# One half of the first layer's modulation: from VectorE dot products to TensorE matmuls

## The chip, the cores and the metric

The kernel runs on one core of one Trainium2 chip (trn2). Times are device microseconds of one execution of the program. The kernel before was timed in three runs: 722.38 us median, 721.82 to 723.79. One further execution was recorded by the hardware profiler. Engines: TensorE (PE, its weight loads PEld), VectorE (DVE), ScalarE (ACT), GpSimd (POOL), and SyncE (SP), whose queue issues nearly all loads here.

## What is computed

Two layers over 256 tokens of width 1024, in fp32: a first layer with a recurrent mixer (hgrn2 and a short convolution), a second with sparse attention, each followed by a gated feed-forward network with a convolution. Every norm is modulated by a vector that comes from a condition `c`:

```python
c_act = jax.nn.silu(c)
for l in range(DEPTH):
    mod = c_act @ mod_w[l] + mod_b[l]
    sh1, sc1, g1, sh2, sc2, g2 = jnp.split(mod[:, None, :], 6, axis=-1)
    hm = rmsnorm(x, norm_mix_g[l]) * (1.0 + sc1) + sh1
...
    x = x + g1 * y
    hf = rmsnorm(x, norm_ffn_g[l]) * (1.0 + sc2) + sh2
    x = x + g2 * conv_ffn(hf, ffn_w_up[l], ffn_conv_w[l], ffn_w_down[l])
return rmsnorm(x, final_norm_g)
```

`mod_w` is 1024 x 6144 for each layer. What the change touches is `sc2` of the first layer: 1024 of these columns.

## The kernel before, in words

Activations are kept transposed: `xT` holds the 1024 features as 8 chunks of 128 partitions by 256 tokens. Every large product is done in three passes of matmuls (`Group.chunk`, L418 to L427, all recorded at L402): each operand is split into a high half (`fp32r`) and a low half, and high x high, low x high and high x low are added. A `Group` makes 256 output features in one PSUM tile `pg`; four chunks of 128 input features are 24 matmuls.

**Weights.** `Stream` reads all weights in the order of use. A dry run of the program writes down the order in which it asks for loads (`load`, L125), and the real run issues them in that order on SP's queue (`_dma`, L117 to L123) as soon as one of 6 buffers of 1 MB is free. Weights (`raw_w`) and modulation matrices (`raw_m`) share these buffers. A weight tile is split in pieces of four chunks: the high half on ScalarE (`whi`, L152), the low half on VectorE (`wlo`, L161), up to three pieces ahead of the matmuls, with four buffers for each half. A buffer is given back after its last low half (`lows`), after the second dot on it, or after the step of matmuls on it (`done`).

**Modulation.** A half is 1024 of the 6144 columns (two quarters of 512). There are two ways to make one:

- `mod_half` (L264 to L300) on TensorE, eight entries: four steps, each with a load of its own of 256 rows of two quarters and four matmuls of 128 x 32 by 512 columns into four column strips of one PSUM tile (`pm`, L283); a copy to SBUF on ScalarE (`mrow`, L289); an empty entry; four transposes (L294); two additions on VectorE (L298, L299).
- `mod_dots` (L302 to L315) on VectorE, eight entries: each one dot product of 128 output columns over all 1024 rows (L311, `raw_m` times `cb`, the condition on every partition). Two share a load.

**Order.** All engines run their instructions in the order of the program text (`manual_schedule`). What is not on the main line is put between: `defer` (L350) hands functions to later slots, and `side` is a list of background entries. `slot(n)` (L357) runs what is due, adds n to a credit of at most 2 and takes entries from `side` while the credit is 1 or more. A slot stands after a piece's splits and before its matmuls. `flush()` runs all that is left.

**The stretch in question**, 108 to 180 us, is the end of the first mixer. `chained` (L799) runs eight groups of the input projection with the recurrence between them. Then four output groups are computed over chunks 4 to 7 (L849 to L856): before each, `o_out(i)` (L782) transposes one head of `on` into the one PSUM tile of tag `a` (`pt`, L785), and after it `finish` forms `og` on VectorE (L789), its high half `ohi` on ScalarE (L790) and its low half `olo` (L791). As `pt` has one buffer, the next transpose waits for `og`. Then the same four groups run over chunks 0 to 3 (L858 to L866), with residuals into `xT` (L542), squares (L479, L481 `sqa`, L489 `sql`) and, in `out_tail` (L544), 24 recorded matmuls of one column each that sum the squares over partitions (L469, `pn`). `fill()` places the first entries of a half of the second layer (`mod_half(1, 0, 1)`) in the gaps: one step before the row sums, one after them, one after the spread of the result (`pb`, L502). Then the feed-forward network starts with the first matmuls on the normed input `hhi` (L513, L514).

Of the kernel before, what the change touches and what calls it, by code (L numbers as in the profile page):

```python
# [195 lines left out]
def model(ctx, tc, xt, pack, wts, rel_bias, k_f, k_mask, k_hot, out, plan, got):  # L196
# [67 lines left out]
    def mod_half(l, qa, qb, tag="m"):  # L264

        def cols(t):
            a = t[:, 4 * qa:4 * qa + 4]
            return bass.AP(tensor=a.tensor, offset=a.offset, ap=[list(a.ap[0]), [4 * (qb - qa), 2], [1, 4]])
        dst, bias = cols(modc[l]), cols(modb[l])
        s_ = {}  # L270

        def load(j):
            s_["i"] = st.load("m", 2048, "mod", l, 2 * j, 2, (512 * qa, 512 * qb), 512)
            return st.raw(s_["i"]).rearrange("p (k n) -> p k n", k=2)

        def pe_step(j):
            raw = load(j)
            if j == 0:
                s_["p"] = ps.tile([P, 512], "pm", tag)
            for e in range(2):  # L280
                for q in range(2):
                    o = 64 * e + 32 * q
                    pe.matmul(s_["p"][o:o + 32, :], cst[:, 2 * j + e, :], raw[:, e, q * 512:(q + 1) * 512],  # L283
                              start=(j == 0), stop=(j == 3), skip_group_check=True, tile_position=(0, o))
            st.done(s_["i"])

        def rows():
            s_["w"] = tmp.tile([P, 512], F32, name="mrow", bufs=1)
            act.activation(s_["w"], s_["p"], AF.Copy)  # L289

        def turn():
            s_["t"] = ps.tile([P, 4, P], "pm2", "m")
            for i in range(4):
                pe.transpose(s_["t"][:, i, :], s_["w"][:, i * P:(i + 1) * P], ident)  # L294

        def add():
            pv = s_["t"].rearrange("p j (e q r) -> p e q j r", q=2, r=32)
            dve.tensor_tensor(dst, pv[:, 0, :, :, 0], bias, op=OP.add)  # L298
            dve.tensor_tensor(dst, pv[:, 1, :, :, 0], dst, op=OP.add)  # L299
        return [lambda j=j: pe_step(j) for j in range(4)] + [rows, nop, turn, add]  # L300

    def mod_dots(l, q):  # L302

        s_ = {}

        def dot(j, e):
            if e == 0:
                s_["i"] = st.load("m", 2048, "dots", l, 512 * q + 256 * j)
            raw = st.raw(s_["i"])[:, e * D:(e + 1) * D]
            n = 4 * q + 2 * j + e  # L310
            dve.tensor_tensor_reduce(raw, raw, cb, scale=1.0, scalar=modb[l][:, n:n + 1], op0=OP.mult, op1=OP.add,  # L311
                                     accum_out=modc[l][:, n:n + 1])
            if e == 1:
                st.done(s_["i"])
        return [lambda j=j, e=e: dot(j, e) for j in range(4) for e in range(2)]  # L315
# [32 lines left out]
    due, side, credit = [], [], [0.0]  # L348
# [444 lines left out]

    chain = [diagonal] + [lambda h=h: level(h) for h in (1, 2, 4, 8, 16, 32, 64)] + [cross, o_products]
    after = [None]
    side.extend(mod_half(0, 4, 5) + mod_dots(0, 6) + mod_dots(0, 8))
    side[:0] = [nop] * 3

    def chained(G):  # L799
# [597 lines left out]
def trace(nc, consts, plan):  # L1397

    args = []
    for name, shape in list(_SHAPES.items()) + [(k, a.shape) for k, a in consts.items()]:  # L1400
        dt = mybir.dt.from_np(consts[name].dtype) if name in consts else F32
        args.append(nc.dram_tensor(f"in_{name}_dram", shape, dt, kind="ExternalInput").ap())
    out = nc.dram_tensor("out_0_dram", (1, S, D), F32, kind="ExternalOutput").ap()
    got = []
    try:
        with tile.TileContext(nc) as tc:
            model(tc, *args, out, plan, got)
    except Traced:
        pass
    return got[0].loads, got[0].subs  # L1410
# [13 lines left out]
```

## Time and profile before

| | us |
|---|---|
| median of three runs (lowest to highest) | 722.38 (721.82 to 723.79) |
| the profiled execution: its own time | 722.53 |
| span in the profile, first to last instruction | 720.8 |
| TensorE busy | 689.8 (96%) |
| VectorE busy | 517.0 (72%) |
| ScalarE busy | 372.9 (52%) |
| mean granted TensorE clock | 0.975 |

A profile is one execution. Busy shares are averages over stages with different limits, so the table of stretches is read before the shares. Matmuls are pipelined: a row's mean duration is longer than the step from one to the next, and the time of a run of them is read from the chain of waits or from the first and the last start. A granted clock of 1.0 is TensorE's level of 2.4 GHz, 0.5 its level of 1.2 GHz. An fp32 matmul of the modulation stands as two records, so a step of four is x8.

### The profile page before, as it was taken

The page shows a single profiled execution, that of the slowest core. Times are in us where ns is not written, and L with a number is a line of the kernel's source. Part 1 is how long each engine was busy: PE and PEld are TensorE (multiplying, and loading weights), DVE is VectorE, ACT ScalarE, POOL GpSimd, SP SyncE. Part 2 cuts the span into 40 slices and gives each one's busy share as a digit, 9 for nine tenths or more (in the row PEclk, how much of TensorE's full clock was granted, in tenths as well). Part 3 has the DMA queues.
Part 4 walks back from the last instruction along what each step waited for, and adds up shares of the span by engine and source line. Part 5 has one row for each costly group of instructions (what it writes and reads, how often), then busy time and mean ns, then how long its engine had stood idle before and what let it go on. Part 6 is the DMA issues. An engine that isn't in the chain of part 4 may idle for free.

```text
span 720.8 us, 14050 instructions
## 1 busy us (share of the span) xinstructions
PE 689.8 (96%) x5730; PEld 651.6 (90%) x5730; DVE 517.0 (72%) x954; ACT 372.9 (52%) x641; POOL 48.2 (7%) x80
## 2 busy tenths in 40 slices
PE   7999999696999999999999999999899999999996
PEld 4889899694999999999989799888799999999996
DVE  3658767866689989985558768788698977665452
ACT  5546245424555555534346668783564555453442
POOL 0000000000000000000010015665000000000000
PEclk9999999896999999999999999999899999999998
DMA  9996835976767878786558592516455865544201
GB/s 326 403 411 241 298 128 171 353 277 235 247 219 270 295 266 321 282 329 205 195 218 318 199 340 75 205 48 234 175 213 211 330 246 185 185 181 162 103 1 60
DMA packets 27793, 165.10 MB, mean 229 GB/s; under 512 B 3258, under 2 KB 3770, under 8 KB 10320
## 3 DMA queue, kind: packets, MB, share of 16 engines
q1 hardware_dynamic: 26352, 159.94, 60.4%
q0 software_dynamic: 944, 3.60, 1.5%
q8 instruction: 45, 0.74, 0.4%
q10 hardware_dynamic: 432, 0.66, 0.3%
q14 instruction: 20, 0.16, 0.1%
HBM read 163.10 MB, written 1.08 MB: 228 GB/s over the span
## 4 chain that ended last, share of the span: by engine, by line
PE 84%; DVE 7%; ACT 5%; DMA 2%; issue 1%; SPq 0%; POOL 0%; ACTq 0%; DVEq 0%
PE pg L402 71%; DVE wlo L161 2%; PE pl L715 2%; ACT whi L152 2%; DVE raw_m L311 2%; PE pm L283 2%; PE pn L469 1%; PE po L1051 1%; PE p L1021 1%; PE pc L1159 1%; PE pm L327 1%; DMA xT<-in_xt_dram 1%; PE sc L973 1%; DMA raw_w<-in_wts_dram 1%; ACT E L1005 1%
## 5 line engine op out<-in xcount | busy, mean ns | idle before, releaser
L161 DVE TENSOR_TENSOR wlo<-raw_w,whi 128x1024 fp32r<-128x1024 f32 (+1 forms) x194 | 227.0, 1176 | 118.5 <-ACT whi L152 117.4
L402 PE MATMUL pg<-hhi,whi 128*128 128x256 f32 x1096 | 296.1, 285 | 1.5 <-ACT hhi L514 1.3
L402 PE MATMUL pg<-hlo,whi 128*128 128x256 f32 x1096 | 291.2, 280 | 0.0
L402 PE MATMUL pg<-hhi,wlo 128*128 128x256 f32 x1096 | 287.9, 279 | 0.0
L152 ACT ACTIVATE whi<-raw_w 128x1024 fp32r<-128x1024 f32 (+1 forms) x194 | 195.4, 1016 | 147.6 <-PE pg L402 123.7
L402 PEld LDWEIGHTS pg<-hhi,whi 128*128 128x128 f32 x1096 | 199.9, 189 | 13.2 <-issue 6.7
L402 PEld LDWEIGHTS pg<-hlo,whi 128*128 128x128 f32 x1096 | 200.4, 189 | 0.0
L402 PEld LDWEIGHTS pg<-hhi,wlo 128*128 128x128 f32 x1096 | 197.6, 188 | 0.0
L402 PE MATMUL pg<-Ah,whi 128*128 128x256 f32 x352 | 99.7, 283 | 0.0
L402 PE MATMUL pg<-Ah,wlo 128*128 128x256 f32 x352 | 99.6, 283 | 0.0
L402 PE MATMUL pg<-Al,whi 128*128 128x256 f32 x352 | 98.7, 280 | 0.0
L311 DVE CUSTOM_DVE_ANT_0 raw_m<-raw_m,cb,pk 128x1024 f32<-128x1024 f32 x56 | 70.9, 1276 | 0.0
L402 PEld LDWEIGHTS pg<-Al,whi 128*128 128x128 f32 x352 | 67.0, 190 | 0.0
L402 PEld LDWEIGHTS pg<-Ah,whi 128*128 128x128 f32 x352 | 66.1, 188 | 0.0
L402 PEld LDWEIGHTS pg<-Ah,wlo 128*128 128x128 f32 x352 | 65.8, 187 | 0.0
L1012 POOL TENSOR_SCALAR E<-E,rr,gr 128x128 f32<-128x128 f32 (+1 forms) x64 | 41.3, 656 | 30.7 <-DVE rr L1010 22.0
L887 DVE SCALAR_TENSOR_TENSOR tt<-pg,pk,tt 128x255 f32<-128x255 f32 (+1 forms) x88 | 36.2, 473 | 2.9 <-ACT tt L883 2.9
L897 ACT ACTIVATE Ah<-tt 128x512 fp32r<-128x512 f32 x22 | 13.9, 633 | 46.2 <-DVE tt L896 46.2
L514 ACT ACTIVATE hhi<-xn,modc 128x256 fp32r<-128x256 f32 x31 | 15.1, 505 | 26.0 <-DVE xn L513 26.0
L1005 ACT ACTIVATE E<-E,mx 128x128 f32<-128x128 f32 (+1 forms) x64 | 28.2, 446 | 0.0
L889 ACT ACTIVATE tt<-tt 128x512 f32<-128x512 f32 x22 | 13.9, 633 | 15.0 <-DVE tt L887 14.6
L1086 POOL MEMSET bls<- 128x128 f32 x1 | 0.2, 204 | 310.8 <-PE pg L402 310.8
(231 smaller groups left out, 795.0 us busy)
## 6 DMA issues: line engine op xcount, KB each, us to landing
raw_w<-in_wts_dram SPq DMA_DIRECT2D x84, 1024.0 KB, 4.9
raw_m<-in_wts_dram SPq DMA_DIRECT2D x52, 1024.0 KB, 6.1
raw_e<-in_wts_dram SPq DMA_DIRECT2D x24, 256.0 KB, 9.0
raw_w<-in_wts_dram SPq DMA_DIRECT2D x8, 768.0 KB, 5.2
FDM<-ub POOLq DMA_DIRECT2D x4, 800.0 KB, 7.3
raw_w<-in_wts_dram SPq DMA_DIRECT2D x5, 512.0 KB, 5.6
xT<-in_xt_dram SPq DMA_DIRECT2D x3, 256.0 KB, 6.5
out_dram<-yo ACTq DMA_DIRECT2D x2, 256.0 KB, 2.9
```

Of the source, the lines that this page charges most:

```text
L152: self.nc.scalar.activation(hi, raw, AF.Copy)
L161: self.nc.vector.tensor_tensor(lo, raw, hi, op=OP.subtract)
L283: pe.matmul(s_["p"][o:o + 32, :], cst[:, 2 * j + e, :], raw[:, e, q * 512:(q + 1) * 512], start=(j == 0), stop=(j == 3), skip_group_check= ...
L311: dve.tensor_tensor_reduce(raw, raw, cb, scale=1.0, scalar=modb[l][:, n:n + 1], op0=OP.mult, op1=OP.add, accum_out=modc[l][:, n:n + 1])
L402: pe.matmul(o, a, b, start=self.first[i], stop=False, skip_group_check=True)
L514: act.activation(hi[:, k, :], xs[k], AF.Identity, bias=B[:, k:k + 1])
L715: pe.matmul(pp[:, hd, :], lhs[:, hd, ls * P:(ls + 1) * P], rhs[:, hd, rs * P:(rs + 1) * P], start=True, stop=True)
L887: dve.scalar_tensor_tensor(tt[:, m, d:], acc[:, m, :S - d], w_fc[l][:, c:c + 1], tt[:, m, d:], op0=OP.mult, op1=OP.add)
L889: defer(taps, lambda: act.activation(tt, tt, AF.Silu))
L897: act.activation(Ah[:, sl, :], tt, AF.Copy)
L1005: act.activation(o, o, AF.Exp, bias=E["mx"][:, t, br:br + 1], scale=-1.0, accum_out=E["den"][:, t, br:br + 1])
L1012: pool.tensor_scalar(o, o, rr[:, t, br:br + 1], gr4[:, t, 1 + br, n:n + 1], op0=OP.mult, op1=OP.mult)
```

## The change

The second half of modulation made in this stretch, quarters 8 and 9 of the first layer (columns 32 to 39 of `modc0`, `sc2`), goes from `mod_dots` to `mod_half`:

```diff
@@ -793,7 +793,7 @@
 
     chain = [diagonal] + [lambda h=h: level(h) for h in (1, 2, 4, 8, 16, 32, 64)] + [cross, o_products]
     after = [None]
-    side.extend(mod_half(0, 4, 5) + mod_dots(0, 6) + mod_dots(0, 8))
+    side.extend(mod_half(0, 4, 5) + mod_dots(0, 6) + mod_half(0, 8, 9))
     side[:0] = [nop] * 3
 
     def chained(G):
```

Both fill eight entries of `side` (one of the new eight is empty), at the same slots. Three places show what moves.

VectorE, over the output groups (`wlo` is the low half of a weight piece, `og` the head that the transposes wait for); minus is before, plus the change:

```order
 L161 TENSOR_TENSOR wlo<-raw_w,whi 128x1024
-L311 ISA raw_m,modc_81<-raw_m,cb,pk 128x1024
-L311 ISA modc_81 128x1
 L789 SCALAR_TENSOR_TENSOR og<-pt,pk,sg 128x256
 L791 TENSOR_TENSOR olo<-og,ohi 128x256
```

A dot stood between the low half and `og` of each of the four heads; it is gone four times, and four more dots are gone between there and `sqa` (two ahead of the first residual, one behind each of the first two residuals).

TensorE, at the same place, ahead of each head's transpose:

```order
 L402 MATMUL pg<-hhi,whi 128x256
 L402 MATMUL pg<-hlo,whi 128x256
 L402 MATMUL pg<-hhi,wlo 128x256
+L283 MATMUL pm<-raw_m,cst 32x512 x4
 L785 MATMUL pt<-kf,on 128x128 x2
 L402 MATMUL pg<-ohi,whi 128x256
```

A step of four matmuls now stands ahead of each of the four transposes; the four transposes of `mrow` (L294) stand behind the first group of the second round, its two additions on VectorE behind the first residual.

SP's queue of loads, before (`raw_w_1379` and `raw_w_1448` hold the weights of the four output groups for chunks 4 to 7, `raw_w_1514` and `raw_w_1585` those for chunks 0 to 3, 1738 and 1742 the first of the feed-forward network):

```order
L121 DMA raw_m_1387<-in_wts_dram 128x2048
L121 DMA raw_w_1448<-in_wts_dram 128x2048
L121 DMA raw_m_1453<-in_wts_dram 128x2048
L121 DMA raw_w_1514<-in_wts_dram 128x2048
L121 DMA raw_m_1518<-in_wts_dram 128x2048
L121 DMA raw_m_1550<-in_wts_dram 128x2048
L121 DMA raw_w_1585<-in_wts_dram 128x2048
L121 DMA raw_m_1625<-in_wts_dram 128x2048
L121 DMA raw_m_1662<-in_wts_dram 128x2048
L121 DMA raw_m_1701<-in_wts_dram 128x2048
L121 DMA raw_w_1738<-in_wts_dram 128x2048
L121 DMA raw_w_1742<-in_wts_dram 128x2048
```

The same places of the queue with the change (`raw_w_1453`, 1550, 1585, 1677 and 1718 are now the five weight loads):

```order
L121 DMA raw_m_1387<-in_wts_dram 128x2048
L121 DMA raw_m_1448<-in_wts_dram 128x2048
L121 DMA raw_w_1453<-in_wts_dram 128x2048
L121 DMA raw_m_1514<-in_wts_dram 128x2048
L121 DMA raw_m_1518<-in_wts_dram 128x2048
L121 DMA raw_w_1550<-in_wts_dram 128x2048
L121 DMA raw_w_1585<-in_wts_dram 128x2048
L121 DMA raw_m_1593<-in_wts_dram 128x2048
L121 DMA raw_m_1634<-in_wts_dram 128x2048
L121 DMA raw_m_1671<-in_wts_dram 128x2048
L121 DMA raw_w_1677<-in_wts_dram 128x2048
L121 DMA raw_w_1718<-in_wts_dram 128x2048
```

The number and the size of the loads are the same. The weights of the third and fourth output group are one place later, those of the second round's first two groups two places later, and all four loads of the half come before them.

## Rows read from the trace of the kernel before

**Rows 1.** The page's part 1: engine, busy us (share of span), instructions.

```profile
PE 689.8 (96%) x5730; PEld 651.6 (90%) x5730; DVE 517.0 (72%) x954; ACT 372.9 (52%) x641; POOL 48.2 (7%) x80
```

**Rows 2.** Busy time by stretch; the columns are named in its first line.

```profile
core 0: us, PE busy (x) PEld busy (x) DVE busy (x) ACT busy (x) POOL busy (x), PEclk, DMA share, GB/s
112.00:138.00 26.00, 19.66 (x169) 19.46 (x167) 22.84 (x33) 12.79 (x23) 0.00 (x0) 0.96 0.71 257
```

**Rows 3.** Waits, 104 to 182 us: who waited for whom: total us, times, longest.

```profile
PE pt L785 <- DVE og L789: 7.3, 2, 6.3
...
PE pn L469 <- DVE sqa L481: 6.0, 1, 6.0
```

**Rows 4.** Chain of waits, 128 to 148 us: start us, us, what.

```profile
136.33 1.20 DVE raw_m L311
...
137.99 0.69 PE pt L785 x2
138.68 4.58 PE pg L402 x23
```

**Rows 5.** The same chain over the whole span, end of the mixer and on.

```profile
156.62 6.15 DMA raw_w<-in_wts_dram
...
165.97 1.19 DVE raw_m L311
...
168.96 5.28 PE pn L469 x24
174.24 1.86 PE pm L283 x8
...
178.59 15.09 PE pg L402 x120
...
203.48 165.11 PE pg L402 x1392
```

**Rows 6.** Groups by shape, 104 to 180 us: x count | busy us, mean ns | idle before.

```profile
L152 ACT ACTIVATE whi<-raw_w 128x1024 fp32r<-128x1024 f32 x16 | 16.5, 1049 | 9.6 <-PE pg L402 6.9 <-DMA raw_w<-in_wts_dram 2.7
...
L311 DVE CUSTOM_DVE_ANT_0 raw_m<-raw_m,cb,pk 128x1024 f32<-128x1024 f32 x16 | 20.3, 1277 | 0.0
L161 DVE TENSOR_TENSOR wlo<-raw_w,whi 128x1024 fp32r<-128x1024 f32 x16 | 19.6, 1223 | 12.3 <-ACT whi L152 12.3
...
L789 DVE SCALAR_TENSOR_TENSOR og<-pt,pk,sg 128x256 f32<-128x256 f32 x4 | 1.9, 478 | 0.0
```

**Rows 7.** The chain, 64 to 93 us, where another half runs on TensorE.

```profile
69.81 2.83 PE pg L402 x24
...
81.14 1.00 PE pm L283 x8
82.14 3.03 PE pg L402 x24
```

**Rows 8.** SP's timeline and DMA issues: one issue; KB each, us to landing.

```profile
124.05 0.33 SPq L121 DMA_DIRECT2D raw_w<-in_wts_dram  x1
...
raw_w<-in_wts_dram SPq DMA_DIRECT2D x15, 1024.0 KB, 4.8
```

**Rows 9.** Busy time by stretch, for granted clock, DMA share and GB/s (columns as rows 2).

```profile
135.90:142.60 6.70, 4.61 (x22) 4.61 (x23) 5.29 (x9) 1.74 (x3) 0.00 (x0) 0.50 0.93 377
131.00:151.00 20.00, 12.74 (x89) 12.34 (x88) 16.17 (x24) 4.70 (x8) 0.00 (x0) 0.83 0.84 317
142.70:166.50 23.80, 19.37 (x162) 18.12 (x160) 16.29 (x25) 7.88 (x10) 0.00 (x0) 1.00 0.71 257
166.60:180.20 13.60, 11.24 (x50) 7.57 (x51) 8.04 (x20) 5.28 (x10) 0.00 (x0) 0.50 0.70 250
518.20:524.90 6.70, 4.72 (x22) 4.27 (x22) 4.09 (x10) 3.96 (x7) 0.00 (x0) 0.50 0.01 2
```

**Rows 10.** The chain, 365 to 375 us, at the second norm.

```profile
369.59 0.98 PE pn L469 x8
...
373.04 1.96 PE pg L402 x14
```

## The prediction

> **What bounds the kernel now.** Read the engines' shares first: TensorE is busy 96% of the span [rows 1], so whatever keeps TensorE waiting, or makes it slow, is what can be won, and whatever is added to TensorE costs in full wherever it never waits. The change touches one stretch, so the second view is the table of busy time by stretch. From 112 to 138 us it is busy 19.7 of 26 us, and VectorE 22.8 of 26 [rows 2]. There the bound is VectorE. The table of waits says for what: TensorE's transposes of `on` (L785) waited 7.3 us for `og` on VectorE, 6.3 of it at once, and the row sums of the norm (L469) 6.0 us for the sum of squares `sqa`, also VectorE's [rows 3].
>
> The chain of waits shows the first of these: a dot product of 1.2 us stands right ahead of `og`, and the transpose starts at 137.99; behind it the 24 matmuls of one output group take 4.58 us [rows 4], where 24 take 2.83 at full rate [rows 7]. The reason is the clock: granted 0.50, the 1.2 GHz level, from 135.9 to 142.6 us, after TensorE had stood idle for 6 us [rows 3, 9].
>
> The second is the end of the stage: a weight load lands after 6.15 us, at 162.77; VectorE works through low halves, residuals and one more dot to `sqa`; the row sums start at 168.96 and, with the steps behind them, run at half clock until the feed-forward's first matmul at 178.59 [rows 5, 9]. From there on TensorE hardly waits (165 us without a pause from 203.5 us on alone [rows 5]), so a start earlier by x ends the kernel earlier by x, as long as weights keep up.
>
> **What it removes.** Eight dots of 1.277 us, 10.2 us of VectorE [rows 6]. The diff of VectorE's order shows them where the two waits end: one ahead of each `og`, two ahead of the first residual, two more ahead of `sqa`. The first and the last of these are in the chains above.
>
> **What it adds.** Four steps of four matmuls (L283). A step takes 1.00 us at full clock, and the 24 matmuls behind one take 3.03 in place of 2.83, so 1.2 us each [rows 7], 4.8 together, about 9 at half clock, where a step takes 1.86 [rows 5]. Four transposes add 0.7 us (an estimate: two take 0.69 at half clock [rows 4]). ScalarE gets one copy of 512 columns and VectorE two additions on eight columns, under 1 us, both beside waits for weights. The steps wait for their own loads, with the output groups queued behind them; the first two go out by 124.05 us, the next two, once their buffers are free, by my reckoning before 131 us, each 6 us or more ahead of use. Nothing moves on POOL.
>
> **What it moves.** The queue of loads matters most. Each step takes a whole load where two dots shared one, so `raw_m_1448` is now issued at 124.05 us [rows 8], ahead of the weights of output groups 2 and 3 (now 1453), and 1514 and 1518 go ahead of `raw_w_1550`, the weights of the second round's first two groups, which stand two places later than before. In exchange buffers come free when TensorE has used them, not when VectorE has got round to them, so the queue does not run dry. Nothing in the trace shows how fast nine loads in a row land. A load is 1.049 MB. While the queue was full it moved 377 GB/s (2.78 us a load), over the stretch from 131 to 151 us 317 GB/s (3.31) [rows 9]. I take the middle, 3.05, because even there the queue had holes, and keep both for the range. A lone load lands 4.8 us after its issue [rows 8].
>
> The Trainium skill, "DMA: Bandwidth & Descriptors", section Bandwidth, has 425 GB/s for a long transfer, faster than these rows; by that a load would take 2.47 us and the sum below would end at about 710.5, where TensorE's own work becomes the limit. The rows show 377 at best.
>
> **The sum.** (1) `raw_m_1448` lands at 124.05 + 4.8 = 128.9 us and `raw_w_1550`, four places later, at 141.05. Its split on ScalarE (1.05), the low half (1.22) and `og` (0.48) [rows 6] give the third transpose about 143.9; the first `og`, now without its dot, is at 136.5, so it does not decide. (2) One group (2.9), one step (1.2), the transposes (0.5): the fourth group starts at 148.5. It and the four of the second round are 120 matmuls, at 2.83 per 24 [rows 7] 14.2 us, and the added transposes 0.4 to 0.7: TensorE ends about 163.2. Now it ends at 162.0 (168.96, less the wait of 6.0 [rows 3], less one step of 1.0), one microsecond earlier. So the 7.3 us of waiting for `og` is filled by steps and by a wait for weights, and wins nothing itself. (3) The last load this stage needs, 1718, is ten places behind 1448: 128.9 + 30.5 = 159.35 (now 162.77). From landing to the row sums it takes 6.2 us today, with one dot in it [rows 5]; without it 5.0, so 164.4, when TensorE is free. (4) 24 row sums at full clock: three times the 0.98 of eight [rows 10] plus 0.5 for the last squares, 3.4. (5) From the end of the row sums to the first matmul 2.5 us, as in the second norm (369.59 + 0.98 to 373.04 [rows 10]), which has the same step between. First matmul: 170.3, against 178.59: 8.3 us. (6) If the clock stays up, the matmuls after it, at half until 180.2 us today, give back 0.8. Sum −9.1. The profiled execution took 722.53 us, 0.15 over the median of the runs: **713.4 us**. With 2.78 us a load it is 711.9 (TensorE's end then nearly binds), with 3.31 it is 715.8. If the cover of step (2) were gone, that is if loads were early and TensorE never waited, the 5.5 us of added matmuls would stand bare there, but the end of the stage would still be set by (3) to (5).
>
> **Rival A: the clock falls all the same.** Between the fourth group's end and the feed-forward lie some 7 us in which TensorE has row sums of one column, three steps and two transposes. In the second norm such a gap of 4.5 us with three steps passed at full clock [rows 10]; before 518.2, with row sums and no steps, it fell to half [rows 9]. Seven microseconds with three steps lie between the two. If it falls, two steps, the transposes and row sums lose about 2, the first matmuls 1.6 more: 3.5, **716.9 us**. The Trainium skill, "TensorE: Matmul & The Clock Gate", section HAM oscillation, says that waits between bursts of matmuls send the clock down again and the next burst starts cold; by that rule this rival is the case, and the second norm speaks against it only for the shorter gap.
>
> **Rival B: the loads turn into the bound, and it gets slower.** Were a load to take 4.08 us, the 257 GB/s of 142.7 to 166.5 us [rows 9], 1718 would land at 169.7, the first matmul come at 180.6, 2 us later than now: **724.5 us**. It decides from 3.97 us a load (first matmul at 178.59). For it: the stage's second round waits for weights today, and the change puts four modulation loads ahead of them. Against it: in that stretch DMA was busy only 0.71 of the time, because buffers were held by dots that now go.
>
> **Rival C: no change.** The steps take as much of TensorE as the dots gave back, 5.5 us plus half clock twice: 720 to 724. For it: TensorE is the fullest engine. Against it: TensorE waits 13 us in this very stretch [rows 3]. That the change does not do what it says is excluded by the order: all eight dots are gone and four steps stand in their place.
>
> **How the numbers follow.** Forecast (clock stays up) 0.49, A 0.36, B 0.07, C 0.08. The likeliest gives 713.4. Its own bounds are 711.9 and 715.8; A's, with the same loads, 715.4 to 719.3. The range 711 to 719 holds nearly all of both; B and C and the tails lie outside, under 2 in 10. About 0.3%, 2.2 us, is what a measurement of this kernel can tell from no change; faster by more is the forecast and A with a little taken off, 0.86; C splits: same 0.06, and slower 0.08 with B.
>
> **What would show it.** Right: VectorE has no L311 rows between 136 and 168 us; TensorE's wait for `og` before the second transpose shrinks to about 3 us and one of 1 to 2 us appears before the third, ended by a load; TensorE ends the fourth group near 163 us; the row sums start near 164.4 and not 169; the feed-forward's first matmul comes near 170 at full clock; the 165 us of matmuls behind it are as long as before. Rival A shows as a granted clock of 0.5 around 167 to 174 us. Wrong: the row sums still start after 168 us because the splits of 1677 and 1718 wait for loads longer than now (B), or feed-forward matmuls that wait for weights and hand back the lead.

## The result, and the profile after

| | before | change |
|---|---|---|
| median, us (lowest to highest, runs) | 723.09 (721.82 to 724.66, 4) | 716.43 (713.61 to 717.11, 4) |
| ratio of the two, 95% interval | | 0.990 (0.9865 to 0.9934) |
| the profiled execution: time, span | 722.53, 720.8 | 717.11, 715.3 |
| mean granted clock of the profiled execution | 0.975 | 0.983 |

The kernel is 6.7 us faster. The forecast said 713.4 (711 to 719): the sign and the range hold, the number is 3.0 us too low and lies near rival A's 716.9. In the experiments below, the ratios leave out one slow execution (722.44 us, run 1), which stands in that run's median and range.

The page's part 1 of the change, then its busy time by stretch (columns as in [rows 2]):

```profile
PE 693.2 (97%) x5766; PEld 650.8 (91%) x5766; DVE 507.7 (71%) x940; ACT 373.7 (52%) x642; POOL 48.4 (7%) x80
```

```profile
core 0: us, PE busy (x) PEld busy (x) DVE busy (x) ACT busy (x) POOL busy (x), PEclk, DMA share, GB/s
112.00:138.00 26.00, 23.00 (x194) 20.99 (x194) 21.71 (x32) 12.91 (x20) 0.00 (x0) 1.00 0.75 277
136.00:142.60 6.60, 4.24 (x34) 3.21 (x34) 1.84 (x3) 1.47 (x2) 0.00 (x0) 1.00 1.01 425
131.00:151.00 20.00, 14.43 (x119) 11.39 (x118) 11.93 (x19) 7.45 (x11) 0.00 (x0) 1.00 1.00 419
142.70:166.50 23.80, 23.27 (x191) 21.34 (x191) 14.80 (x27) 11.04 (x15) 0.00 (x0) 0.98 0.66 255
165.50:172.20 6.70, 6.70 (x30) 3.03 (x30) 2.73 (x8) 2.72 (x6) 0.00 (x0) 0.50 0.98 402
510.30:520.40 10.10, 8.12 (x38) 7.67 (x37) 6.17 (x13) 4.84 (x9) 0.00 (x0) 0.50 0.01 2
```

Against [rows 2, 9]: TensorE is busy 23.0 of the 26 us up to 138 (19.7 before) and 23.3 of the 23.8 up to 166.5 (19.4). The loads run at 419 GB/s from 131 to 151 us (317). The granted clock is 1.00, the 2.4 GHz level, where it was 0.50 at 136 to 142.6 us; it is 0.50 at 165.5 to 172.2 (before 166.6 to 180.2), and for 10 us at the third norm (before 6.7).

The waits from 104 to 182 us (total, times, longest):

```profile
ACT whi L152 <- DMA raw_w<-in_wts_dram: 6.1, 2, 3.7
PE pt L785 <- DVE og L789: 5.6, 2, 3.0
```

The transposes still wait 5.6 us, in pieces of 3.0 and 2.6 where they were 6.3 and 1.0; the wait of the row sums for `sqa` [rows 3] is gone. The chain of waits of the change:

```profile
131.31 9.05 DMA raw_w<-in_wts_dram
...
141.55 1.23 DVE wlo L161
142.78 0.41 DVE og L789
...
143.23 0.44 PE pt L785 x2
143.66 2.81 PE pg L402 x24
...
147.84 5.70 PE pg L402 x48
...
153.98 8.54 PE pg L402 x72
162.52 0.99 PE pm L283 x8
163.52 3.41 PE pn L469 x24
166.93 1.86 PE pm L283 x8
...
169.41 1.87 PE pm L283 x8
171.28 14.81 PE pg L402 x120
...
196.20 165.11 PE pg L402 x1392
```

From the third transpose at 143.23 to the long run of matmuls at 196.20 every link is TensorE's own work. The feed-forward starts at 171.28 and not 178.59 [rows 5]: a lead of 7.31 us. It is 7.28 at the start of the long run of matmuls (196.20 against 203.48) and 7.28 at the second norm's first matmul (365.76 against 373.04 [rows 10]). At the third norm part of it is handed back. The change there, then the kernel before, from the same chain over the whole span:

```profile
509.73 3.18 PE pn L469 x16
...
515.53 148.43 PE pg L402 x1236
...
696.93 10.09 PE pg L402 x84
```

```profile
516.74 2.33 PE pn L469 x16
...
521.69 147.69 PE pg L402 x1236
...
702.37 10.10 PE pg L402 x84
```

The lead is 7.01 at the row sums, 6.16 at the matmul behind them and 5.44 at the end: 1.6 us go where the granted clock is 0.50 for longer.

### The profile page after: what moved, and what is told of

Same layout as the page of the kernel before. It is cut to its first block, busy times and chain, and to the rows that moved or that the text cites. A ratio compares the mean times of both kernels' runs of the same rounds, so it can differ in the third digit from the quotient of the medians.

```text
span 715.3 us, 14109 instructions
## 1 busy us (share of the span) xinstructions
PE 693.2 (97%) x5766; PEld 650.8 (91%) x5766; DVE 507.7 (71%) x940; ACT 373.7 (52%) x642; POOL 48.4 (7%) x80
## 4 chain that ended last, share of the span: by engine, by line
PE 87%; DVE 4%; ACT 4%; DMA 2%; issue 1%; POOL 0%; SPq 0%; ACTq 0%; DVEq 0%
PE pg L402 74%; PE pl L715 2%; PE pm L283 2%; DVE wlo L161 2%; ACT whi L152 1%; PE pn L469 1%; DMA raw_w<-in_wts_dram 1%; PE po L1051 1%; PE p L1021 1%; PE pc L1159 1%; PE pm L327 1%; DMA xT<-in_xt_dram 1%; PE sc L973 1%; ACT E L1005 1%; PE pw L610 0%
## 5 line engine op out<-in xcount | busy, mean ns | idle before, releaser
L311 DVE CUSTOM_DVE_ANT_0 raw_m<-raw_m,cb,pk 128x1024 f32<-128x1024 f32 x48 | 60.8, 1275 | 0.0
L897 ACT ACTIVATE Ah<-tt 128x512 fp32r<-128x512 f32 x22 | 13.9, 633 | 46.5 <-DVE tt L896 46.5
L514 ACT ACTIVATE hhi<-xn,modc 128x256 fp32r<-128x256 f32 x31 | 15.1, 505 | 26.0 <-DVE xn L513 26.0
L889 ACT ACTIVATE tt<-tt 128x512 f32<-128x512 f32 x22 | 13.9, 634 | 14.7 <-DVE tt L887 14.4
```

The lines of the kernel that those rows point to most:

```text
L514: act.activation(hi[:, k, :], xs[k], AF.Identity, bias=B[:, k:k + 1])
L889: defer(taps, lambda: act.activation(tt, tt, AF.Silu))
L897: act.activation(Ah[:, sl, :], tt, AF.Copy)
```

## The experiments

Each group of runs was timed beside the kernel before on the same chip, whose median there was 723.99 (runs 1 to 4), 724.42 (5 to 8) and 722.35 (9 to 12).

| | kernel | median, us (range) | ratio to before, 95% | minus before, us |
|---|---|---|---|---|
| 1 | eight dots thinned | 717.12 (710.88 to 722.44) | 0.9835 to 0.9943 | -6.9 |
| 2 | first four thinned | 721.78 (718.53 to 723.57) | 0.9955 to 1.0008 | -2.2 |
| 3 | last four thinned | 721.56 (716.78 to 722.98) | 0.9938 to 0.9989 | -2.4 |
| 4 | change, steps twice | 716.87 (715.26 to 717.61) | 0.9865 to 0.9940 | -7.1 |
| 5 | change, pairs share a load | 713.68 (710.77 to 715.98) | 0.9822 to 0.9887 | -10.7 |
| 6 | change, halves swapped | 728.11 (723.22 to 729.41) | 1.0023 to 1.0076 | +3.7 |
| 7 | change, clock held | 716.79 (715.21 to 717.54) | 0.9870 to 0.9920 | -7.6 |
| 8 | change, squares folded | 719.41 (713.40 to 720.31) | 0.9911 to 0.9961 | -5.0 |
| 9 | change, split later (last three) | 715.13 (710.51 to 716.63) | 0.9846 to 0.9902 | -7.2 |
| 10 | change, split later (all four) | 712.13 (707.09 to 715.46) | 0.9812 to 0.9873 | -10.2 |
| 11 | before, split later (all four) | 722.50 (720.37 to 726.70) | 0.9986 to 1.0032 | +0.2 |
| 12 | change again | 717.14 (712.04 to 719.17) | 0.9869 to 0.9935 | -5.2 |

The profiles of runs 3 and 8 went through the second feed-forward 4 us quicker than the others did (last section), so the totals of these two executions say less than the medians.

**Runs 1 to 3: how much of it is VectorE's relief?** The kernel before, with the dots of quarters 8 and 9 cut to the first 8 of 1024 rows; all eight, only quarter 8's four, only quarter 9's four. Loads and order stay as before. Run 1:

```diff
-            dve.tensor_tensor_reduce(raw, raw, cb, scale=1.0, scalar=modb[l][:, n:n + 1], op0=OP.mult, op1=OP.add,
-                                     accum_out=modc[l][:, n:n + 1])
+            w = 8 if (l, q) == (0, 8) and j < 4 else D
+            dve.tensor_tensor_reduce(raw[:, :w], raw[:, :w], cb[:, :w], scale=1.0, scalar=modb[l][:, n:n + 1], op0=OP.mult,
+                                     op1=OP.add, accum_out=modc[l][:, n:n + 1])
```

Run 2 has `j < 2` there, run 3 `j >= 2`.

> The kernel before, with the eight dots of quarters 8 and 9 cut to their first 8 of 1024 rows (the sums are no longer the modulation; loads, order and buffers as before, no steps on TensorE). Theory: it is VectorE's time that held the stretch, and with it gone TensorE's own work is the bound; the loads come at 2.5 us each and do not hold it. TensorE ends the fourth group of the second round near 160 us (162.0 before, 162.5 with the change), the feed-forward starts near 168.5: 713 to 715 us, so the steps and the new order of loads cost the change 2 to 3 us. Rival 1 (buffers): the gain comes from buffers that TensorE frees early, not from VectorE's time; then this is 720 or more. Rival 2: the added steps are bare; then this is 5 us under the change, 711.5 or less.

> The kernel before, with only the four dots that stand ahead of the four heads (quarter 8) cut to 8 rows; the four of quarter 9 stay. Theory: the long wait for the first head shrinks by one dot only, since VectorE has five other dots and its low halves ahead of it, so TensorE ends the second round 1 to 2.5 us earlier and the end of the stage, set by the remaining dots and loads, follows: 720 to 721.5 us. Rival: the 7.3 us of waiting for og are the gain; then this gives 5 or more, 717 or less, and the other four dots little.

> The kernel before, with only the four dots between the last head and the sum of squares (quarter 9) cut to 8 rows; the four ahead of the heads stay. Theory: the end of the stage is where the time is; TensorE ends as before at 162, but the feed-forward's weights are issued earlier and the sum of squares is ready 4 us or more earlier, so the row sums follow the fourth group at once: 715 to 717.5 us. Rival: without the earlier heads nothing moves; 720 or more.

Run 1 gave as much as the change (717.12, above the 713 to 715 expected), and both parts alone about a third each (run 2's interval includes no change), so neither chain is worth much while the other stands. That the last four would give most was wrong. The chain of run 1 shows what I had excluded (lines are one higher from L311 on):

```profile
144.10 14.09 PE pg L403 x120
...
162.67 0.61 DVE sqa L482
...
163.32 5.08 PE pn L470 x24
```

TensorE is through its matmuls at 158.19, 31.1 us after the end of the input projection (127.13); in the change it takes 34.4 (128.17 to 162.52). But the row sums then wait 4.2 us for `sqa`, and the feed-forward starts at 172.75 and not near 168.5. ScalarE's timeline says why:

```profile
155.53 1.06 ACT L152 ACTIVATE whi<-raw_w 128x1024 fp32r<-128x1024 f32 x1 [7.31 <-DMA raw_w<-in_wts_dram]
```

That load was issued at 149.50 only, right behind the low half that gave its buffer back. In the change the same weights go into another buffer, are issued at 145.86, and no split waits for them. So VectorE's relief does not act alone: the tail also needs the loads that follow buffers freed earlier. By the order of the queue this load, like the one that lands at 162.77 in the kernel before [rows 5], holds weights of the feed-forward network. What stands on ScalarE and VectorE ahead of the last residuals and `sqa` is thus the split of weights that TensorE needs only behind the norm. Putting that split behind `sqa` was not tried.

**Run 4: what do the steps cost TensorE?** Every step's matmuls twice.

```diff
+            for r in range(2 if (l, qa) == (0, 8) else 1):
                 for e in range(2):
```

> The change, with each of its four steps of matmuls done twice (the sums are doubled; loads and order as with the change). Theory: the first three steps stand ahead of waits (for the first head, and for the weights of the second round), so doubling them is hidden; the fourth is on the path and costs 1.0 to 1.2 us: 717 to 718 us, TensorE's end 1 us later. Rival: TensorE is the bound all through; four steps more cost 4 to 5 us: 720.5 or more.

Four times 0.86 us more of TensorE's work cost nothing that the medians show. The doubled steps of 1.85 us (0.99 in the change) in part filled waits (2.3 us are left of 5.6); TensorE ended 1.6 us later after the end of the input projection (1 us was expected), but the row sums and the step behind them then ran at full clock. So the price is small but hidden by the clock, not nil: the one execution with a mean clock of 0.990 took 715.26 us, where the change took 712.04 and 712.43 at 0.990. The chain (lines one higher from L280 on):

```profile
142.46 1.85 PE pm L284 x16
...
165.39 2.77 PE pn L470 x24
168.16 0.99 PE pm L284 x8
```

**Run 5: is the wait before the third transpose one for weights?**

```diff
-            raw = load(j)
+            if (l, qa) != (0, 8):
+                raw = load(j)
+            elif j % 2 == 0:
+                raw = s_["r"] = load(j)
+            else:
+                raw = s_["r"]
```

> The change, but each two of the half's four steps use one load (two loads of 1 MB fewer; the steps of the second and fourth multiply the rows of the first and third, so the modulation is not the reference's). It moves the weights of the second round's first two groups (1550 before) up by two places, some 5 us. Theory: the wait of about 2.6 us before the third transpose in the changed kernel is a wait for these weights, as the prediction's step (1) has it; it goes, TensorE ends the second round 2 to 2.5 us earlier (relative to the first transpose 32 rather than 34.4), and the feed-forward starts at most that much earlier: 714.0 to 715.0. Rival: the tail is set by the loads of the last two groups, which depend on buffers and not on places in the queue: TensorE is free earlier, the row sums start no earlier, 716.4 as the changed kernel.

The theory holds: TensorE ended the second round 31.8 us after the end of the input projection (34.4 in the change). The median, 713.68, came out a little below the 714.0 expected. Two transposes waited in the change; here one does (the table of waits; lines six higher):

```profile
PE pt L791 <- DVE og L795: 3.0, 1, 3.0
```

The clock stayed at 1.00 from 17 to 508 us, so the tail ran at full rate as well. 2 MB of loads less is nothing a real kernel can have, but the wait it removes can go in another way (runs 9 and 10).

**Run 6: place or number?** The steps and the remaining dots change places.

```diff
-    side.extend(mod_half(0, 4, 5) + mod_dots(0, 6) + mod_half(0, 8, 9))
+    side.extend(mod_half(0, 4, 5) + mod_half(0, 8, 9) + mod_dots(0, 6))
```

> The change's three halves with the last two swapped: the steps of quarters 8 and 9 run beside the recurrence and the last input groups, and the eight dots of quarters 6 and 7 take the slots around og and sqa. The same work on every engine as in the changed kernel. Theory (what counts is that the dots left the chains of og and sqa): both waits of TensorE for VectorE come back, the steps cost 4.8 us where TensorE has no gap, 723 to 728. Rival (what counts is that VectorE has 10 us less to do in all): 716.4 as the changed kernel.

Same work on every engine, some 10 us slower than the change and slower than before. The number of dots is not what counts. Two things add up. The steps stand bare where TensorE has no gap: the first transpose starts at 133.67, 4.5 us later than in the change (129.17). And the wait for `sqa` is back; that for `og` is not (2.9 us in three pieces), against the expectation. TensorE's longest wait from 104 to 184 us, and the load that the chain shows ahead of it:

```profile
PE pn L469 <- DVE sqa L481: 10.9, 1, 10.9
```

```profile
162.06 4.68 DMA raw_w<-in_wts_dram
```

ScalarE's splits wait 13.9 us for loads here (6.1 in the change), so this run does not part VectorE's own time from buffers that come back late.

**Run 7: is the clock what the forecast missed?**

```diff
+            def stay():
+                if keep is not None:
+                    for _ in range(6):
+                        pe.matmul(keep[:, :S], G.X[0][:, 0, :P], G.X[0][:, 0, :], start=True, stop=True)
```

It is called twice among the first norm's row sums.

> The change with 12 more matmuls of 128 x 128 by 256 columns whose result nobody reads, six before and six in the middle of the first norm's row sums, to hold TensorE's clock there. Theory (rival A of the prediction is what the changed kernel lost against the forecast): granted clock 1.0 from 160 us to the feed-forward; the 12 cost 1.4 us, two steps, the transposes and the spread at full clock give back 3: 714.5 to 715.5. Rival: the clock falls all the same or the loss was elsewhere: 717.5 to 718.5.

The total is a miss, between the two bands: no gain that can be told from the change. In the stretch itself it did much as expected (the chain; L567 is the added work):

```profile
165.52 0.98 PE pn L469 x8
166.50 0.82 PE pk L567 x6
...
172.19 13.94 PE pg L402 x120
```

Row sums to first matmul take 6.67 us with 1.64 of added matmuls in them; the change takes 7.76. The clock was at 0.50 twice as long near 12 us in this profile, ahead of anything edited, and the first transpose came 1.8 us later (130.98 against 129.17), which more than took the 1.1 us back. That is one execution; why the median of five is no lower than the change's is open.

**Run 8: fewer row sums?**

```diff
-FOLD = (False, True, False, True)
+FOLD = (True, True, False, True)
```

> The change with the squares of the first norm added over the chunks on VectorE, as in the second and fourth norms, so that 8 row sums stand where 24 stood. Theory (VectorE has room again since the dots left; TensorE's own work ends the stage): the row sums take 1 us rather than 3.4, less what VectorE adds at the last chunk, 714 to 715. Rival: the additions put VectorE back at the end of the stage, as the dots did; the row sums start 1 to 3 us later and nothing is won: 716 to 718.

The rival's mechanism holds: VectorE's additions are late in place of the dots, and 16 row sums less win nothing (719.41 us, even above its band of 716 to 718). The table of waits:

```profile
PE pn L469 <- DVE sqa L557: 3.2, 1, 3.2
```

**Runs 9 to 11: the split out of the way.** VectorE's timeline of the change around the second `og`:

```profile
135.88 0.48 DVE L789 SCALAR_TENSOR_TENSOR og<-pt,pk,sg 128x256 f32<-128x256 f32 x1
...
141.55 1.23 DVE L161 TENSOR_TENSOR wlo<-raw_w,whi 128x1024 fp32r<-128x1024 f32 x1 [4.28 <-ACT whi L152]
142.69 0.48 DVE L789 SCALAR_TENSOR_TENSOR og<-pt,pk,sg 128x256 f32<-128x256 f32 x1
```

VectorE is idle for 4.28 us and then makes the low half of weights that TensorE needs at about 150.7 us, with the `og` that it needs at once behind it. So the wait for weights (prediction's step 1) is one of order on VectorE. Run 10 (run 9 has `min(i, 1)` for the 1; run 11 is run 10's edit on the kernel before):

```diff
-        s_ = G[i].sub(4, 4)
+        s_ = G[i].sub(4, 4, 1)
```

> The change, with the split of weight pieces running two pieces ahead rather than three in the last three output groups, so that the low half of the second round's first piece stands behind og of the second head on VectorE and not ahead of it. All work is done; the queue of loads is the same. Theory: the 2.6 us before the third transpose is og standing in VectorE's queue behind the split of weights that TensorE does not need yet; the load itself is early enough. Third transpose at most 0.5 us after TensorE is ready, TensorE ends the second round 2 to 2.6 us earlier relative to the first transpose (32 rather than 34.4), median 713.5 to 715. Rival: the wait moves into the second round, because the splits are now late there, or the row sums wait for VectorE as in the thinned dots: 716.4.

> As split_later, but two pieces ahead in all four output groups: the low half of the second load's second piece also goes from ahead of the first og to behind it. Theory: the second transpose too comes 1.1 us earlier (its wait 1.9 rather than 3.0 us), 712.5 to 714. Rival: VectorE and the tail of the stage set the end, no more than split_later.

> The kernel before, with the same later split in the four output groups; the eight dots stay on VectorE. Theory: VectorE is full there and the end is set by its whole queue and by the last weight loads, so one low half less ahead of og wins at most 1 us: 722.5 to 724. Rival: the later split by itself is worth as much as on the changed kernel: 720.5 to 721.5.

Run 10 beats both kernels in its median: 10.2 us under before, 5 under the change beside it (ratios to before 0.9843 and 0.9902; their intervals just overlap at 0.987). Its chain has one wait for `og`, of 2.1 us, and a tail at full clock:

```profile
135.88 0.69 PE pt L785 x2
136.57 4.00 PE pg L402 x24
...
141.57 0.37 PE pt L785 x2
...
160.84 0.99 PE pm L283 x8
161.83 2.77 PE pn L469 x24
...
167.07 13.94 PE pg L402 x120
```

Not all of the 5 us is the wait. From the end of the input projection to the row sums run 10 takes 33.3 us (128.52 to 161.83), 2.0 less than the change; 2.5 more come from the tail, which runs at full clock here (5.24 us from row sums to first matmul, 7.76 in the change). The timed executions say the same: at like mean clocks (0.980, 0.988, 0.990) run 10 is 1.0 to 2.7 us under the change, and the rest goes with a clock that was higher in most of its executions. That the edit keeps the clock up is not shown.

Run 9's median of 715.13 lies in neither band and its interval reaches the change's ratio; in its profile the clock fell at 137 us and the second group took 5.12 us, which covers the wait in question, so it tells little alone. Run 11 wins nothing: on the kernel before, the same edit moves no end. In its profile the transposes wait 5.9 us for `og` (7.3 before) and the row sums 9.5 us for `sqa` (6.0), so what the heads win the tail seems to give back.

**Run 12: the change again.**

> The changed kernel once more, beside the three others, for its spread: 716.4 median, single runs 713.5 to 717.5; the granted clock of the whole run 0.981 to 0.988, with 0.5 in a part of the tail of the first mixer or none, and in the third norm, as it falls.

The median agrees, the spread is wider than expected on both sides. In this profile the clock fell at 137 us too, and the wait before the third transpose was gone, filled by a group at half clock:

```profile
139.13 5.01 PE pg L402 x24
144.14 0.99 PE pm L283 x8
145.13 0.37 PE pt L785 x2
...
165.40 3.02 PE pn L469 x24
168.41 1.86 PE pm L283 x8
```

From the end of the input projection to the row sums it takes 35.4 us in the first profile of the change (128.17 to 163.52) and 35.5 in this one (129.89 to 165.40).

## Why the prediction was right, and where it was off

**The bound was read rightly.** VectorE ahead of two waits [rows 3, 4, 5], not the shares of the whole span. Run 1 shows that taking VectorE's work away is worth as much as the change, run 4 that the steps' own price here is small, run 6 that the place decides. What part of it is VectorE's own time and what part buffers given back earlier, no run tells apart.

**Step (1)** said 141.05 for `raw_w_1550`, third transpose 143.9: measured 140.36 and 143.23. Run 5 shows this wait to be worth some 2.6 us of TensorE's time, run 10 that it stands there through the order on VectorE.

**Step (2)** said that TensorE's matmuls end at 163.2, a microsecond later than before, and that filling the wait for `og` wins nothing by itself: 162.52 against 162.0.

**Step (3) is the mis-sized term.** It held the middle of 2.78 and 3.31 us a load, so that the last load lands at 159.35 and the row sums start at 164.4 behind it. In the full queue a load took 2.47 to 2.50 us (1.049 MB at 425 and 419 GB/s). No split waited for the last loads, and the row sums began at 163.52 because TensorE itself was done; the case that the text gave to 2.78 us and below. The last load, 1718, was issued at 147.53 and landed 7.7 us later, at 155.2: the step was 4.1 us too late, of which 0.9 reached the row sums. The 3.05 us came from rows of the kernel before, whose queue had holes. Nor does the stage need 1718 for itself: it holds weights of the feed-forward network, whose split stands ahead of `sqa`.

The Trainium skill, "DMA: Bandwidth & Descriptors", section Bandwidth, has 425 GB/s for a transfer of 16 MB and 341 for one of 1 MB, both issued from GpSimd. The trace agrees with the first for loads of 1 MB one behind the other on SP's queue (425 from 136 to 142.6 us). "377 at best" was a matter of the window: from 136.0 to 140.5 us, with a DMA share of 0.99, the kernel before moved 401 GB/s. A full share alone does not settle the rate: run 1 moved 363 GB/s at a share of 1.00 from 133 to 139.8 us, and why is open.

**Step (4)** said 3.4 us for the row sums at full clock. The 3.41 measured agrees by luck, as part of it ran at half clock; at full clock they took 2.77 (run 10).

**Step (5), 2.5 us to the first matmul, failed:** 171.28 - 166.93 = 4.35, with the two steps at 1.86 and 1.87 us. That is rival A as the prediction had it, and **step (6)**, 0.8 us back, did not come: the lead of 7.31 us at the first matmul is 7.28 at 196.20. Together with step (3) the first matmul came at 171.28 in place of 170.3.

**What no step had:** the third norm, far from the edit. There 1.6 us of the lead went with a longer stretch of half clock. 7.3 less that and 0.3 before it is the 5.4 by which the profiled executions differ. So it is in part luck that the total lies near rival A's 716.9: the tail and step (6) cost 1.8 us against the forecast, where A had 3.5, and 1.9 us were lost far behind, where A had nothing.

The Trainium skill, "TensorE: Matmul & The Clock Gate", section HAM oscillation, speaks for rival A, with waits between bursts as its cause. Both profiles of the change agree as to the clock, 0.50 from 165.5 and from 167.8 us; but TensorE had not waited since 143 and 138 us, and run 10's tail, with the same matmuls and the same row sums, kept 1.00. What decides it is open. In the ten timed executions of the change, three with a mean clock of 0.988 to 0.990 took 712.0 to 713.6 us, near the forecast, and seven with 0.976 to 0.983 took 716.2 to 719.2, near rival A; which stretch made the difference is known for the two profiled ones alone. The clock also enters the 6.7 us: at a mean clock of 0.976 the change took 719.05 and 719.17 us, and the kernel before 721.7 to 723.9 in all but one execution (718.27), so some 3 us of the gain stand at like clock and the rest goes with a higher one.

**Rivals B and C** are out: loads ran faster and not slower, and the row sums' wait is gone. Two sums of the prediction are off by its own terms, without effect: B decides from 3.88 us a load and not 3.97, and 3.31 us a load gives 716.0 and not 715.8.

## What to carry to other kernels

Work that is moved from one engine to another pays by the wait that it stood in front of: eight dots given back for steps were worth -6.7 us in one place and +3.7 in another, where the steps stood bare. After such a move, look at what else stands in an in-order queue ahead of the result that the bound engine waits for; here the split of a weight tile not yet needed held TensorE up by some 2 us (5 in the medians, clock included), and moving it won nothing before the move. Price a load from a stretch in which the queue had buffers to fill (2.47 to 2.50 us here) and not from one with holes (2.78 to 3.31).

## What was not expected of the hardware

The second feed-forward runs at two paces, though no edit touches it. Run 8's profile, beside 148.43 us of the change for the same matmuls at the same granted clock of 1.00 (but for the first 5 to 6 us, in both):

```profile
516.00 144.23 PE pg L402 x1236
```

Run 3's took 144.07; the other profiles have the long one. Counted from start to start, 100 matmuls take 11.78 us in the one and 11.33 in the other, for some 1000 matmuls on end without a wait. What sets the pace was not tried. Some timed executions lie as far under others of like clock (707.09 us of run 10 at 0.986, beside 713.26 and 713.51); that they have the quick pace is not shown.

The clock at half cost nothing where TensorE would have waited anyway: run 12's group of 5.01 us against 2.81 ended where the wait would have (third transpose 15.2 us after the end of the input projection, 15.1 in the first profile of the change).
